# Last norm through VectorE's block transposes, a third output chunk on GpSimd, and other transfer prices in the ordering model

## The chip, the core and the metric

The kernel runs on one core of one Trainium2 chip. The core has five engines that run side by side, each with its own queue of instructions: PE (TensorE, matmuls into PSUM), DVE (VectorE), ACT (ScalarE), POOL (GpSimd) and SP (SyncE, which here issues nearly all transfers). They wait for each other through semaphores. The metric is the device time of one execution in microseconds; less is better.

## What is computed

Two layers of an encoder trunk on 512 tokens of width 1024, and a last RMSNorm. Cut to the parts that matter here:

```python
def rms_norm(x, g):
    x32 = x.astype(jnp.float32)
    y = x32 * lax.rsqrt(jnp.mean(x32 * x32, axis=-1, keepdims=True) + EPS)
    return (y * g.astype(jnp.float32)).astype(x.dtype)
...
    for l in range(DEPTH):
        x = x + hybrid_mixer(rms_norm(x, norm_mix[l]), ...)
        x = x + memory_cross_attention(rms_norm(x, norm_mem_q[l]), rms_norm(mem, norm_mem_kv[l]), ...)
        x = x + conv_ffn(rms_norm(x, norm_ffn[l]), w_up[l], conv_w[l], conv_b[l], w_down[l])
    return rms_norm(x, norm_final)
```

The mixer has neighbourhood attention and grouped-query attention side by side; conv_ffn ends in a product with w_down, 2816 by 1024. Everything is float32 outside; the products are made of three float32r products of high and low parts (mm3).

## The kernel before

The residual x is kept transposed: eight tiles xT of 128 channels by 512 tokens. A product is a run of matmuls of 128 by 128 weights on up to 512 columns. Weights come from memory into two "raw" buffers, are split into a high part (ACT) and a low part (POOL or DVE), and wait in four buffers until PE uses them. In the attention parts, the keys of two heads are doubled by a transfer inside the SBUF (line 998, "r<-r" in the profile), ahead of the scores that use them.

**The order.** The program does not run in the order in which it is written. Every instruction is first put on a tape (class Tape, lines 156 to 382); the tape knows what each one reads and writes. `plan` (line 344) then simulates the five engines with prices of its own: matmuls and elementwise work by columns (`times`, line 109), a transfer by 450 ns to issue it, its bytes by one of three rates (line 96), and LANDING, 1500 ns, until its result may be used (line 317). Each engine takes the step that is due first among those that can start soon; PE may run ahead of its written order by up to 300 steps. Three settings with three rounds each give nine orders. Each is then run again three times with random delays on every step (line 360), and the order with the best mean is played. So every engine's order, that of SP's queue too, follows from these prices. On the chip the queues are strictly in order: a step whose operand is late holds all behind it on its engine.

**A norm.** The squares of the eight chunks are summed on ACT and DVE or POOL into `acc`. Every norm but the last goes through `totals` (line 698): DVE transposes `acc` in blocks of 32 by 32, reduces within blocks, and PE adds across with the constant matrix `sel`; `by_block` scales in four pieces of 32 partitions, POOL takes the power -1/2 (`rsqrt`) and lays the values out with a mask (`apart`); later `along` multiplies with `sel` once more and DVE transposes the result, repeated, into a tile as wide as the tokens (`rep`).

The last norm has its own way. Its eighth square is kept apart (`last`, line 780), `stat` sums `acc` and `last` by matmuls with a column of ones (line 794), three blocks of 128 tokens each, and `spread` calls `row_rep` (line 737): three matmuls of the repeated scale with the identity give the wide tile in PSUM, and ACT copies it to the SBUF as `rep` for POOL, which does not read PSUM.

**The end** (`down_last`, lines 1595 to 1671). The first 384 tokens end in transposed layout, the last 128 ("tail") in rows of tokens. PE first makes all eight chunks for the 384 tokens; then two closing products of 512 columns for the tail, `pms[0]` and `pms[1]`. The norm's `stat` is written between their parts, `spread` after `pms[0]`. Eight multiplications by the wide scale follow, chunks 2 and 5 on POOL from `rep`, the others on DVE from PSUM, and after each one SP issues its output. Behind the last closing matmul come ACT's square with its sum, DVE's variance `v`, POOL's power `rstd`, the scaling of the two halves of `y` on DVE and ACT, and one output from each of SP and ACT.

Of the kernel before, what the change touches and what calls it, by code (L numbers as in the profile page):

```python
# [11 lines left out]
F32 = mybir.dt.float32  # L12
F32R = mybir.dt.float32r
AF = mybir.ActivationFunctionType
ALU = mybir.AluOpType
# [38 lines left out]

ENGINES = range(5)
E_PE, E_ACT, E_DVE, E_POOL, E_SP = ENGINES
HANDOVER, LANDING, IN_FLIGHT, GRACE = 40.0, 1500.0, 8, 140.0
IN_PSUM = ("mm", "sc", "tr")
TWO_INPUTS = ("tensor_add", "tensor_sub", "tensor_mul", "tensor_tensor", "scalar_tensor_tensor")
FAST = ("tensor_scalar", "tensor_copy")  # L60
# [15 lines left out]
class Step:  # L76
# [5 lines left out]
    def __init__(self, i, engine, name, call, args, kwargs):  # L82
        self.i, self.engine, self.name, self.call = i, engine, name, (call, args, kwargs)
        self.reads, self.writes = [], []
        for n, a in [*enumerate(args), *kwargs.items()]:
            if hasattr(a, "tensor") or type(a).__name__ == "Tile":
                a = a if hasattr(a, "ap") and not callable(a.ap) else a[:]
                (self.writes if n in (0, "out", "accum_out") else self.reads).append(a)
        self.needs, self.frees, self.after, self.leads = set(), set(), set(), set()
        self.opens, self.tiles, self.moved = [], [], 0  # L90
        if name == "dma_start":
            self.busy = self.length = 450.0
            to, source = self.writes[0], self.reads[0] if self.reads else None
            short = min(4 * a.ap[-1][1] for a in (to, source) if a is not None) < 1024
            inside = source is not None and type(source.tensor).__name__ == type(to.tensor).__name__ == "Tile"
            rate = 215.0 if to.shape[0] < P or inside else 300.0 if short else 370.0
            self.moved = 4 / rate
            for c in to.shape:
                self.moved *= c
        elif name == "make_identity":  # L100
            self.busy = self.length = 1200.0
        else:
            self.busy, self.length = self.times()
        ends = self.reads[:: max(1, len(self.reads) - 1)] if name in TWO_INPUTS else self.reads[:1] + self.writes
        self.shared = engine == E_POOL and columns(self.writes[0]) > 8 or (
            engine == E_DVE and (name in TWO_INPUTS or name in FAST and (name == "tensor_copy" or columns(self.writes[0]) > 4))
            and all(tag_of(a.tensor) not in IN_PSUM for a in ends))
# [48 lines left out]
class Tape:  # L156
# [84 lines left out]
    def run(self, due, rank, patience, ahead, margin=0.0, aside={}, order=None, rng=None):  # L241
# [32 lines left out]
        for _ in steps:  # L274
# [39 lines left out]
            end = t + busy + s.length - s.busy + late[i]  # L314
            if s.moved:
                memory = max(memory, t + busy) + s.moved
                end = memory + LANDING + 12.0 * late[i]
                flying.append(end)
            taken.append(i)
            open_to[s.engine].remove(i)  # L320
# [23 lines left out]
    def plan(self, log=None):  # L344

        n = len(self.steps)
        best = None
        for patience, ahead, margin, aside, rounds in PLANS:
            rank, at, now = list(range(n)), [0.0] * n, 0.0
            for s in self.steps:  # L350
                at[s.i] = now
                now += s.busy * (s.engine == E_PE)
            for _ in range(rounds):
                r = self.run(self.due(at, rank), rank, patience, ahead, margin, aside)
                if r is None:
                    if log:
                        log("stuck")
                    break
                at = r[1]
                under = [self.run(None, rank, (0.0,) * 5, 0, order=r[2], rng=np.random.default_rng(k)) for k in range(3)]  # L360
                mean = sum(u[0] if u else 1e9 for u in under) / len(under)
                if log:
                    log(r[0], mean)
                if best is None or mean < best[0]:
                    best = mean, r[2]
        return best[1]
# [104 lines left out]
def encoder_kernel(ctx: ExitStack, tc: tile.TileContext, t: dict, out: list):  # L471
# [16 lines left out]
    def nm(s):  # L488
        uid[0] += 1
        return f"{s}_{uid[0]}"  # L490
# [15 lines left out]
    def tmp(shape=(S,)):  # L506
        return tpool.tile([P, *shape], F32, tag="t", name=nm("t"))

    def small(n):
        return spool.tile([P, n], F32, tag="s", name=nm("s"), padded_shape=[P, 16])  # L510
# [184 lines left out]
    mhalf = cpool.tile([P, 8], F32, name="mhalf")  # L695
    DVE.memset(mhalf, -0.5)

    def totals(acc, n):


        t = tmp((n,))
        DVE.transpose(t, acc)
        part = small(n // 32)
        DVE.tensor_reduce(part, t.rearrange("p (j c) -> p j c", c=32), axis=AX.X, op=ALU.add)
        pv = ps_t()
        PE.matmul(pv[:, 0 : n // 32], sel, part, start=True, stop=True)
        return pv[:, 0 : n // 32]

    def by_block(v, nb, op):


        for a in range(4):
            q = slice(32 * a, 32 * a + 32)
            op(q, v[q].rearrange("p (b a) -> p a b", a=4)[:, a])
# [15 lines left out]
    def along(rep, e, n):  # L730
# [2 lines left out]
        pr = ps_t()[:, 0 : n // 32]  # L733
        PE.matmul(pr, sel, e, start=True, stop=True)
        DVE.transpose(rep.rearrange("p (j c) -> p j c", c=32), pr.unsqueeze(2).to_broadcast([P, n // 32, 32]))

    def row_rep(rstd, n, tag, bufs, copy):

        pr = ps_t()
        for b in range(n):  # L740
            PE.matmul(pr[:, b * P : (b + 1) * P], rstd[:, b : b + 1].to_broadcast([P, P]), ident,
                      start=True, stop=True)
        rep = tpool.tile([P, n * P], F32, tag=tag, name=nm(tag), bufs=bufs)
        copy(rep, pr[:, : n * P])
        return rep, pr[:, : n * P]

    class Norm:

# [39 lines left out]
        def stat(self, factor=1.0):  # L788
            nb = self.n // P

            def sums(sq):
                pv = ps_t()
                for b in range(nb):
                    PE.matmul(pv[:, b : b + 1], sq[:, b * P : b * P + P], ones, start=True, stop=True)
                return pv[:, 0:nb]

            if self.last is None:
                pv = totals(self.acc, self.n)
                self.var = small(nb)
                by_block(pv, nb, lambda q, x: DVE.tensor_scalar(  # L800
                    self.var[q], x, factor / D, EPS * factor, op0=ALU.mult, op1=ALU.add))
                self.rstd = rsqrt(self.var, nb)
                if self.gcol != G_MQ:
                    self.wide = apart(self.rstd, nb)
                return

            part, v, self.rstd = small(nb), small(nb), small(nb)
            DVE.tensor_scalar(part, sums(self.acc), 1.0 / D, EPS, op0=ALU.mult, op1=ALU.add)
            DVE.scalar_tensor_tensor(v, sums(self.last), 1.0 / D, part, op0=ALU.mult, op1=ALU.add)
            POOL.tensor_tensor(self.rstd, v, mhalf[:, :nb], op=ALU.pow)  # L810

        def spread(self):
            if self.last is None:
                self.rep = tpool.tile([P, self.n], F32, tag="rep", name=nm("rep"), bufs=1)
                along(self.rep, self.wide, self.n)
            else:
                self.rep, self.psum = row_rep(self.rstd, self.n // P, "rep", 1, ACT.copy)

    def split_psum(hi, lo, ps, scale=None):
        if scale is None:  # L820
# [45 lines left out]
    def mem_stat():  # L866

        acc = None
        for i in range(KC // 2):
            sq = tmp((2, MEMN))  # L870
            SP.dma_start(sq, t["memT"][i * 256 : (i + 1) * 256, :].rearrange("(k p) n -> p k n", p=P))
            yield
            ACT.activation(sq, sq, AF.Square)
            if acc is None:
                acc = sq
            else:
                POOL.tensor_add(acc, acc, sq)
        POOL.tensor_add(acc[:, 0], acc[:, 0], acc[:, 1])
        yield
        v = small(MB)  # L880
        by_block(totals(acc[:, 0], MEMN), MB, lambda q, x: DVE.tensor_scalar(
            v[q], x, 1.0 / D, EPS, op0=ALU.mult, op1=ALU.add))
        yield
        POOL.tensor_tensor(mem_rstd, v, mhalf[:, :MB], op=ALU.pow)
        along(mem_rep, apart(mem_rstd, MB), MEMN)
        yield
# [31 lines left out]
    for l in range(DEPTH):  # L918
# [676 lines left out]
        def down_last(g):  # L1595
# [60 lines left out]
            norm.spread()  # L1656
            for k in range(KC):
                xk = xT[k][:, cs]
                if k in (2, 5):
                    POOL.tensor_mul(xk, xk, norm.rep)  # L1660
                else:
                    DVE.tensor_mul(xk, xk, norm.psum)
                SP.dma_start(out[0][k * P : (k + 1) * P, :], xk)
# [1 line left out]
            squares(1)  # L1665
            DVE.tensor_scalar(v, sums[:, 1:2], 1.0 / D, part0, op0=ALU.mult, op1=ALU.add)
            POOL.tensor_tensor(rstd, v, mhalf[:, :1], op=ALU.pow)
            DVE.tensor_scalar(y[:, 0], y[:, 0], rstd, 1.0, op0=ALU.mult, op1=ALU.mult)
            SP.dma_start(out[1][:, 0:512], y[:, 0])
            ACT.activation(y[:, 1], y[:, 1], AF.Copy, scale=rstd)  # L1670
            ACT.dma_start(out[1][:, 512:D], y[:, 1])

        for g, (j0, nj) in enumerate(GROUPS):
            for j in range(j0 + (g > 0), j0 + nj):
# [99 lines left out]
```

## Time and profile before

| | us |
|---|---|
| median of three runs | 1327.1 |
| lowest and highest of them | 1326.02, 1327.68 |
| the profiled execution | 1326.05 |
| its span, first to last instruction | 1324.3 |
| TensorE's granted clock in it | 0.999 |

The profile is one execution. Its engines are named PE (matmuls), PEld (weight loads, beside PE), DVE, ACT, POOL and SP; a "q" behind a name is the engine's sequencer, which issues transfers. An entry such as "mm<-r,hi 128x512 x8" is a group of instructions by the names of the tiles that they write and read, with the shape and the count. All recorded work has line 376, where the tape is played, so groups are told apart by tiles. In a view by time the first number is the start in microseconds and the second the time until the group's last instruction ends; what stands in brackets is the idle time before it and what ended it. PE's ends are modelled: neighbouring matmuls overlap in the view, and the distance from one start to the next is the time that PE was held.

### The profile page before, as it was taken

What the parts mean: (1) busy time and instruction counts of PE and PEld (TensorE: products, weight loads), DVE (VectorE), ACT (ScalarE), POOL (GpSimd) and SP (SyncE); (2) the same over time, 40 slices, a digit from 0 to 9 for tenths busy, and PEclk for the clock granted to TensorE, in tenths of its full rate; (3) what the DMA queues carried; (4) which work ended last, traced back from release to release, by engine and by line L of the source; (5) the groups of instructions that cost most, each with busy time, mean ns of one, the idle gap of its engine ahead of it and who ended that gap; (6) DMA issues with size and microseconds to landing.
All of it is one profiled execution on the core that took longest, in us unless ns stands there. A gap on an engine that the chain in (4) does not pass through costs nothing.

```text
span 1324.3 us, 17771 instructions
## 1 busy us (share of the span) xinstructions
PE 1315.4 (99%) x6385; PEld 1107.4 (84%) x6385; DVE 931.2 (70%) x1651; ACT 678.8 (51%) x1229; POOL 688.6 (52%) x479
## 2 busy tenths in 40 slices
PE   9999999999999999999999999999999999999998
PEld 8888888888888888888888988888888888888897
DVE  7679895777993388178445898867779815862874
ACT  7776786654442243144437868865644423432441
POOL 3565866737444444444625657765454444444451
PEclk9999999999999999999999999999999999999999
DMA  7751324313333333333355522233143333333331
GB/s 239 217 168 49 96 64 94 98 55 103 97 96 96 96 96 88 106 122 88 99 159 160 144 64 80 72 89 96 48 119 100 99 96 96 92 89 106 96 112 64
DMA packets 198328, 137.29 MB, mean 104 GB/s; under 512 B 5217, under 2 KB 184929, under 8 KB 198241
## 3 DMA queue, kind: packets, MB, share of 16 engines
q1 hardware_dynamic: 197808, 135.77, 35.4%
q8 instruction: 51, 0.84, 0.3%
q10 hardware_dynamic: 432, 0.39, 0.1%
q14 instruction: 37, 0.30, 0.1%
HBM read 126.18 MB, written 2.10 MB: 97 GB/s over the span
## 4 chain that ended last, share of the span: by engine, by line
PE 96%; POOL 2%; DMA 1%; issue 0%; DVE 0%; ACT 0%; SPq 0%; POOLq 0%; ACTq 0%
PE mm L376 85%; PE sc L376 7%; PE tr L376 4%; POOL lo L376 1%; DMA r<-r 1%; POOL r L376 0%; POOL t L376 0%; POOL s L376 0%; DVE r L376 0%; ACT r L376 0%; DVE s L376 0%; ACT t L376 0%; ACT hi L376 0%; SPq L376 0%; DVE t L376 0%
## 5 line engine op out<-in xcount | busy, mean ns | idle before, releaser
L376 POOL TENSOR_TENSOR lo<-raw,hi 128x1024 fp32r<-128x1024 f32 (+2 forms) x268 | 510.0, 1913 | 492.6 <-ACT hi L376 462.5
L376 PE MATMUL mm<-xg,hi 128*128 128x512 f32 (+1 forms) x1730 | 535.0, 390 | 0.0
L376 ACT CAST hi<-raw 128x512 fp32r<-128x512 f32 (+2 forms) x276 | 227.2, 841 | 376.9 <-PE mm L376 341.6
L376 PEld LDWEIGHTS mm<-xg,hi 128*128 128x128 f32 x1730 | 322.4, 188 | 65.2 <-ACT hi L376 0.2
L376 PE MATMUL mm<-xg,lo 128*128 128x512 f32 (+1 forms) x865 | 336.9, 389 | 0.0
L376 PE MATMUL mm<-r,hi 128*128 128x512 f32 (+1 forms) x1056 | 332.7, 390 | 0.0
L376 DVE SCALAR_TENSOR_TENSOR t<-t,par,t 128x504 f32<-128x504 f32 (+1 forms) x352 | 287.7, 854 | 39.6 <-ACT t L376 37.5
L376 PEld LDWEIGHTS mm<-r,hi 128*128 128x128 f32 x1056 | 197.0, 188 | 39.1 <-ACT r L376 0.4
L376 PE MATMUL mm<-r,lo 128*128 128x512 f32 (+2 forms) x560 | 210.9, 377 | 0.0
L376 PEld LDWEIGHTS mm<-xg,lo 128*128 128x128 f32 x865 | 162.5, 188 | 33.8 <-DVE lo L376 0.3
L376 DVE TENSOR_TENSOR xT<-xT,mm 128x512 f32<-128x512 f32 (+1 forms) x56 | 36.9, 667 | 121.5 <-PE mm L376 121.5
L376 PEld LDWEIGHTS mm<-r,lo 128*128 128x128 f32 x560 | 105.2, 188 | 19.4
L376 PE MATMUL mm<-hi,xg 128*128 128x512 f32 (+1 forms) x384 | 108.2, 358 | 0.0
L376 POOL TENSOR_SCALAR t<-t,s 128x512 f32<-128x512 f32 (+1 forms) x112 | 67.0, 613 | 72.5 <-DVE s L376 63.9
L376 PE MATMUL sc<-r,r 128*128 128x256 f32 (+1 forms) x382 | 82.8, 335 | 1.6 <-DMA r<-r 1.6
L376 DVE TENSOR_TENSOR t<-mm,rep 128x512 f32<-128x512 f32 x88 | 60.1, 687 | 31.2 <-PE mm L376 30.9
L376 ACT ACTIVATE t<-sc,s,s 128x512 f32<-128x512 f32 (+1 forms) x96 | 67.8, 710 | 26.4 <-DVE s L376 25.8
L376 ACT ACTIVATE t<-t,par 128x512 f32<-128x512 f32 x88 | 71.3, 813 | 12.3 <-DVE t L376 11.9
L376 PEld LDWEIGHTS mm<-hi,xg 128*128 128x128 f32 x384 | 68.4, 189 | 9.4
L376 PE MATMUL tr<-ident,t 128*128 128x128 f32 x488 | 70.6, 272 | 0.4 <-DVE r L376 0.4
L376 PEld LDWEIGHTS tr<-ident,t 128*128 128x128 f32 x488 | 58.8, 140 | 12.3 <-POOL t L376 0.8
L376 PE MATMUL mm<-lo,xg 128*128 128x512 f32 (+1 forms) x192 | 68.2, 355 | 0.0
(129 smaller groups left out, 1499.4 us busy)
## 6 DMA issues: line engine op xcount, KB each, us to landing
raw<-in_w_up SPq DMA_DIRECT2D x88, 512.0 KB, 3.9
raw<-in_w_in SPq DMA_DIRECT2D x33, 512.0 KB, 4.2
raw<-in_w_down SPq DMA_DIRECT2D x23, 512.0 KB, 3.9
raw<-in_w_down SPq DMA_DIRECT2D x24, 448.0 KB, 3.7
raw<-in_w_mem_kv SPq DMA_DIRECT2D x16, 512.0 KB, 4.0
r<-r SPq DMA_DIRECT2D x30, 256.0 KB, 4.1
r<-in_bias SPq DMA_DIRECT2D x16, 384.0 KB, 6.2
raw<-in_w_out SPq DMA_DIRECT2D x8, 512.0 KB, 3.5
```

Of the source, the lines that this page charges most:

```text
L376: call(*args, **kwargs)
```

## The change

Four edits:

1. The last norm's `stat` uses `totals` like the others. `totals` takes several tiles of squares, transposes and reduces each on DVE, and lets PE add them in one PSUM tile. `spread` uses `along`, into a PSUM tile this time, which ACT then copies to `rep` as before. The matmuls with ones and `row_rep` go.
2. Of the eight last multiplications POOL does chunks 1, 4 and 6 in place of 2 and 5.
3. The last scaling is cut at 640 of 1024 columns in place of 512: DVE and SP's output take 640, ACT and its output 384.
4. In the ordering model LANDING is 1800 in place of 1500, the three rates are 205, 285 and 340 in place of 215, 300 and 370, a trial run adds up to 1500 ns at random to each transfer where it was twelve times a delay of up to 80 ns, and there are six trial runs per order in place of three.

```diff
-HANDOVER, LANDING, IN_FLIGHT, GRACE = 40.0, 1500.0, 8, 140.0
+HANDOVER, LANDING, IN_FLIGHT, GRACE = 40.0, 1800.0, 8, 140.0
...
-            rate = 215.0 if to.shape[0] < P or inside else 300.0 if short else 370.0
+            rate = 205.0 if to.shape[0] < P or inside else 285.0 if short else 340.0
...
-                end = memory + LANDING + 12.0 * late[i]
+                end = memory + LANDING + (12.0 * late[i] if rng is None else 1500.0 * rng.random())
...
-                under = [self.run(None, rank, (0.0,) * 5, 0, order=r[2], rng=np.random.default_rng(k)) for k in range(3)]
+                under = [self.run(None, rank, (0.0,) * 5, 0, order=r[2], rng=np.random.default_rng(k)) for k in range(6)]
...
-    def totals(acc, n):
+    def totals(n, *squares):
...
+        parts = []
+        for sq in squares:
+            t = tmp((n,))
+            DVE.transpose(t, sq)
+            parts.append(small(n // 32))
+            DVE.tensor_reduce(parts[-1], t.rearrange("p (j c) -> p j c", c=32), axis=AX.X, op=ALU.add)
+        pv = ps_t()[:, 0 : n // 32]
+        for i, part in enumerate(parts):
+            PE.matmul(pv, sel, part, start=i == 0, stop=i == len(parts) - 1)
+        return pv
...
-            part, v, self.rstd = small(nb), small(nb), small(nb)
-            DVE.tensor_scalar(part, sums(self.acc), 1.0 / D, EPS, op0=ALU.mult, op1=ALU.add)
-            DVE.scalar_tensor_tensor(v, sums(self.last), 1.0 / D, part, op0=ALU.mult, op1=ALU.add)
-            POOL.tensor_tensor(self.rstd, v, mhalf[:, :nb], op=ALU.pow)
+            pv = totals(self.n, self.acc, *([] if self.last is None else [self.last]))
+            self.var = small(nb)
+            by_block(pv, nb, lambda q, x: DVE.tensor_scalar(
+                self.var[q], x, factor / D, EPS * factor, op0=ALU.mult, op1=ALU.add))
+            self.rstd = rsqrt(self.var, nb)
+            if self.gcol != G_MQ:
+                self.wide = apart(self.rstd, nb)
...
             else:
-                self.rep, self.psum = row_rep(self.rstd, self.n // P, "rep", 1, ACT.copy)
+                self.psum = ps_t()[:, : self.n]
+                along(self.psum, self.wide, self.n)
+                ACT.copy(self.rep, self.psum)
...
-                if k in (2, 5):
+                if k in (1, 4, 6):
                     POOL.tensor_mul(xk, xk, norm.rep)
                 else:
                     DVE.tensor_mul(xk, xk, norm.psum)
...
-            DVE.tensor_scalar(y[:, 0], y[:, 0], rstd, 1.0, op0=ALU.mult, op1=ALU.mult)
-            SP.dma_start(out[1][:, 0:512], y[:, 0])
-            ACT.activation(y[:, 1], y[:, 1], AF.Copy, scale=rstd)
-            ACT.dma_start(out[1][:, 512:D], y[:, 1])
+            yf = y.rearrange("p i n -> p (i n)")
+            DVE.tensor_scalar(yf[:, :640], yf[:, :640], rstd, 1.0, op0=ALU.mult, op1=ALU.mult)
+            SP.dma_start(out[1][:, 0:640], yf[:, :640])
+            ACT.activation(yf[:, 640:], yf[:, 640:], AF.Copy, scale=rstd)
+            ACT.dma_start(out[1][:, 640:D], yf[:, 640:])
```

More of the change, by code (lines that the diff above doesn't have):

```diff
@@ L696, in encoder_kernel @@
     DVE.memset(mhalf, -0.5)
-    def totals(acc, n):
[L701 to L707, printed above, removed]
+    def totals(n, *squares):
[9 more added lines that the diff above has]
+        return pv
     def by_block(v, nb, op):
@@ L735, in along @@
         DVE.transpose(rep.rearrange("p (j c) -> p j c", c=32), pr.unsqueeze(2).to_broadcast([P, n // 32, 32]))
[L737 to L745, printed above, removed]
     class Norm:
@@ L789, in stat, with spread @@
             nb = self.n // P
[L791 to L795, printed above, removed]
-            if self.last is None:
[L798 to L805, printed above, removed]
-            part, v, self.rstd = small(nb), small(nb), small(nb)
-            DVE.tensor_scalar(part, sums(self.acc), 1.0 / D, EPS, op0=ALU.mult, op1=ALU.add)
-            DVE.scalar_tensor_tensor(v, sums(self.last), 1.0 / D, part, op0=ALU.mult, op1=ALU.add)
-            POOL.tensor_tensor(self.rstd, v, mhalf[:, :nb], op=ALU.pow)
-        def spread(self):
-            if self.last is None:
-                self.rep = tpool.tile([P, self.n], F32, tag="rep", name=nm("rep"), bufs=1)
+            pv = totals(self.n, self.acc, *([] if self.last is None else [self.last]))
[5 more added lines that the diff above has]
+                self.wide = apart(self.rstd, nb)
+        def spread(self):
+            self.rep = tpool.tile([P, self.n], F32, tag="rep", name=nm("rep"), bufs=1)
+            if self.last is None:
                 along(self.rep, self.wide, self.n)
             else:
-                self.rep, self.psum = row_rep(self.rstd, self.n // P, "rep", 1, ACT.copy)
+                self.psum = ps_t()[:, : self.n]
+                along(self.psum, self.wide, self.n)
+                ACT.copy(self.rep, self.psum)
     def split_psum(hi, lo, ps, scale=None):
@@ L880, in mem_stat @@
         v = small(MB)
-        by_block(totals(acc[:, 0], MEMN), MB, lambda q, x: DVE.tensor_scalar(
+        by_block(totals(MEMN, acc[:, 0]), MB, lambda q, x: DVE.tensor_scalar(
             v[q], x, 1.0 / D, EPS, op0=ALU.mult, op1=ALU.add))
```

## The prediction

> **What bounds the kernel now.** I read the page first: its span, the busy shares and the chain that ended last; then who PE (TensorE) waits for, the table of equal stretches, the chain around the one long wait, and last the end of the span in order of time.
>
> ```profile
> span 1324.3 us, 17771 instructions
> ...
> PE 1315.4 (99%) x6385; PEld 1107.4 (84%) x6385; DVE 931.2 (70%) x1651; ACT 678.8 (51%) x1229; POOL 688.6 (52%) x479
> ...
> PE mm L376 85%; PE sc L376 7%; PE tr L376 4%; POOL lo L376 1%; DMA r<-r 1%; POOL r L376 0%; POOL t L376 0%; POOL s L376 0%; DVE r L376 0%; ACT r L376 0%; DVE s L376 0%; ACT t L376 0%; ACT hi L376 0%; SPq L376 0%; DVE t L376 0%
> ```
>
> PE is busy in 1315.4 of 1324.3 us, and 96% of the chain is PE by the three PE entries. A microsecond of another engine's work is therefore worth nothing unless PE stands for it or it lies behind the last matmul; a microsecond of PE work is worth one, as long as what follows it keeps pace. PE is not busy in 8.9 us, and this is where they are:
>
> ```profile
> PE sc L376 <- DMA r<-r: 1.6, 1, 1.6
> PE tr L376 <- DVE ones L376: 1.0, 1, 1.0
> PE tr L376 <- DVE r L376: 0.4, 1, 0.4
> ```
>
> ```profile
> 66.22:99.32 33.10, 31.52 (x217) 28.76 (x216) 25.10 (x72) 24.57 (x63) 21.02 (x25) 1.00 0.59 168
> ```
>
> ```profile
> 1305.64 0.53 ACT L376 ACTIVATE t<-xT 128x384 f32<-128x384 f32 x1 [3.11 <-DVE xT L376]
> ...
> 1307.15 1.39 PE L376 MATMUL tr<-ones,t 128*128 128x1 f32 x12
> ...
> 1308.40 0.48 PE L376 MATMUL sc<-hi,r 128*128 128x512 f32 x1
> ...
> 1308.82 0.85 POOL L376 TENSOR_TENSOR s<-s,mhalf 128x3 f32<-128x3 f32 x1 [19.39 <-DVE s L376]
> ...
> 1314.18 0.83 PE L376 MATMUL tr<-ident,s 128*128 128x128 f32 x6
> ...
> 1314.77 3.68 PE L376 MATMUL sc<-r,r 128*128 128x512 f32 x15
> 1315.05 0.48 ACT L376 COPY rep<-tr 128x384 f32<-128x384 f32 x1 [2.26 <-PE tr L376]
> 1315.56 2.88 DVE L376 TENSOR_TENSOR xT<-xT,tr 128x384 f32<-128x384 f32 x6 [1.99 <-ACT rep L376]
> 1315.61 2.00 POOL L376 TENSOR_TENSOR xT<-xT,rep 128x384 f32<-128x384 f32 x2 [5.94 <-ACT rep L376]
> 1316.15 3.85 SPq L376 DMA_DIRECT2D out<-xT  x8
> 1318.48 0.60 ACT L376 ACTIVATE t<-sc 128x512 f32<-128x512 f32 x1 [2.95 <-PE sc L376]
> ...
> 1319.21 0.21 DVE L376 TENSOR_SCALAR s<-s,s 128x1 f32<-128x1 f32 x1 [0.77 <-ACT t L376]
> ...
> 1319.50 0.55 POOL L376 TENSOR_TENSOR s<-s,mhalf 128x1 f32<-128x1 f32 x1 [1.90 <-DVE s L376]
> 1320.09 0.48 DVE L376 TENSOR_SCALAR r<-r,s 128x512 f32<-128x512 f32 x1
> 1320.11 0.72 ACT L376 ACTIVATE r<-r,s 128x512 f32<-128x512 f32 x1 [0.94 <-POOL s L376]
> 1320.60 0.33 SPq L376 DMA_DIRECT2D out<-r  x1
> 1320.87 0.35 ACTq L376 DMA_DIRECT2D out<-r  x1
> ```
>
> The waits of PE sum to 3.0 us: 1.0 at the start for a memset, 1.6 in one matmul of scores for a copy inside the SBUF, 0.4 for a VectorE result. The stretch from 66.22 shows the same hole (33.10 less 31.52 is 1.6 us). The last matmul ends at 1314.77 + 3.68 = 1318.45, and the span's last 5.85 us are the tail: a square with its sum on ScalarE, the variance on VectorE, a power on GpSimd, two scalings side by side, two output transfers and the closing of the program. So 3.0 + 5.85 is the whole of the 8.9. What can be won: work taken from PE, 2.0 us of waits (the start is untouched), and some of the tail.
>
> **Part one, the last norm.** Removed on PE: the sums by a column of ones, twelve instructions that hold PE from 1307.15 to the next matmul at 1308.40, 1.25 us; and the spreading by the identity, six that hold it from 1314.18 to 1314.77, 0.59 us. Added on PE: two matmuls with sel as weights in totals and one in along, each a pair of instructions on 12 columns. The trace has such pairs with 16 columns:
>
> ```profile
> 964.44 0.29 PE L376 MATMUL tr<-s,sel 128*128 128x16 f32 x2
> 964.58 0.71 PE L376 MATMUL mm<-xg,hi 128*128 128x512 f32 x2
> ```
>
> A pair holds PE for 964.58 - 964.44 = 0.14 us, so three hold it for 0.42. The sum is 1.25 + 0.59 - 0.42 = 1.42 us of PE work less. It counts in full only if the new chain does not make PE or the outputs wait, and that chain is longer. Its prices:
>
> ```profile
> L376 DVE STREAM_TRANSPOSE t<-t 128x512 f32<-128x512 f32 x6 | 4.3, 711 | 0.2
> ...
> L376 DVE TENSOR_REDUCE s<-t 128x16 f32<-128x512 f32 x6 | 4.1, 681 | 0.1
> L376 DVE TENSOR_SCALAR s<-tr 32x4 f32<-32x4 f32 x24 | 3.8, 158 | 6.8 <-PE tr L376 6.5
> ...
> L376 DVE STREAM_TRANSPOSE t<-t 128x256 f32<-128x256 f32 x1 | 0.4, 446 | 0.0
> ```
>
> ```profile
> L376 POOL TENSOR_TENSOR s<-s,mask 128x16 f32<-128x16 f32 x4 | 0.9, 218 | 0.3
> ```
>
> A VectorE transpose or reduction of 384 columns is not in the trace; between 446 ns at 256 columns and 711 at 512 I take the middle, 0.58 us for the transpose, and below 0.68 (the 512-column reduction) 0.55 for the reduction. First half, from the last square: ScalarE ends it at 1305.64 + 0.53 = 1306.17; transpose and reduction bring 1307.3 (those of the other seven chunks' sum are done or fit before, since VectorE has little to do there); a pair on PE 1307.6; four small scalings of 32 partitions at 158 ns, 0.63 us, 1308.3; the power on three columns, 0.85 us as at 1308.82, and the masking, 218 ns, 1309.5 with handovers. It is needed when PE comes to the spreading, now 1314.18 less the 1.25 - 0.28 us saved ahead of it, 1313.2. The cover is 3.7 us of product matmuls; both new POOL steps and the eleven or so on VectorE are hidden by it. If the cover were gone, each would cost its own duration, 3.3 us in all after the square.
>
> Second half: the pair ends near 1313.5 with its write; a transpose from PSUM to PSUM, 0.58 us, is new; then the same ScalarE copy as before (0.48), and the multiplications begin at about 1314.65 where they began at 1315.56. They come 0.9 us earlier, while PE's end comes 1.42 earlier, at 1317.03: half a microsecond of slack is spent. Behind them queue the variance on VectorE, the power on GpSimd and, in SyncE's queue, the last output.
>
> **Part two, three chunks on GpSimd.** VectorE did six in 2.88 us, one each 0.46; five end at 1314.65 + 2.4 = 1317.05, and the variance comes at 1319.21 - 1.42 = 1317.8: 0.7 us of cover. GpSimd did two in 2.00 us; three end at 1317.7, and its power is wanted at 1319.50 - 1.42 = 1318.08: 0.4 us of cover. SyncE issues eight transfers in 3.85 us; begun 0.9 earlier, the last ends at 1319.1, where the last output is wanted at 1320.60 - 1.42 = 1319.2. It just fits, so I cost this part at nothing, with a bound of +0.5 (half a microsecond of spent slack) if every one of these estimates is short.
>
> The Trainium skill, Perfetto Trace Analysis, section Optimizing Scalar/DVE Operations, speaks against it: GpSimd's only port is one that VectorE also uses, under a lock, so work moved between these two might gain nothing. The rows do not bear it out for these instructions: the multiplications of both ran at once, six in 2.88 us beside two in 2.00.
>
> **Part three, 640 + 384 columns.** Now VectorE scales 512 in 0.48 us and its transfer is issued at 1320.60; ScalarE takes 0.72 and its transfer is issued at 1320.87, the later one. By columns, 384 on ScalarE are between 0.54 us (in proportion) and 0.72 (no gain); I take 0.62, a tenth less. VectorE's 640 are at most 0.60 in proportion, so its transfer is issued by 1320.72, still before ScalarE's at 1320.77.
>
> ```profile
> out<-r SPq DMA_DIRECT2D x1, 256.0 KB, 2.1
> out<-r ACTq DMA_DIRECT2D x1, 256.0 KB, 2.4
> ```
>
> They land at 1322.7 and 1323.3, so ScalarE's sets the end; an earlier issue and fewer bytes there can win no more than the 0.57 us between the two, and the other one then takes over. Value -0.1 us (the earlier issue alone), from 0 to -0.5. The tail's sum is -1.42 - 0.1 = -1.5 us, bounds -1.42 - 0.5 = -1.9 and -1.42 + 0.5 = -0.9.
>
> **Part four, the ordering model.** The landing price goes from 1500 to 1800 ns and the three rates fall by 5 to 8%; the trial runs are six and put up to 1500 ns of chance on each transfer. Nothing is computed differently, but every engine's order, SyncE's queue included, may come out new in the whole kernel. What the transfers really take:
>
> ```profile
> raw<-in_w_up SPq DMA_DIRECT2D x88, 512.0 KB, 3.9
> ...
> r<-r SPq DMA_DIRECT2D x30, 256.0 KB, 4.1
> r<-in_bias SPq DMA_DIRECT2D x16, 384.0 KB, 6.2
> ```
>
> The old model gives a 256 KB copy 450 + 1500 + 262144 / 215 = 3.17 us, the new one 3.53; the median row says 4.1. For a 512 KB load it was 3.37 and is 3.79; the row says 3.9. So the model came nearer to the rows, and what it places behind a transfer goes later by some 0.4 us. The stall it could mend is this one:
>
> ```profile
> 68.31 3.75 POOL lo L376 x3
> ...
> 72.08 0.37 SPq L376
> ...
> 72.62 7.17 DMA r<-r
> ```
>
> Read in order of time: GpSimd's three splits until 72.06, then the load on SyncE that waited for them, then the copy behind it in the same queue, 7.17 us until it lands, then PE's scores. The copy stood behind a load that waited for a buffer. If it goes ahead of it, or the scores go later among the projections, the 1.6 us vanish. The bounds are -2.0 us (this and the 0.4) and, on the other side, a stall of the same kind made new: 7.17 less the 3.53 that the model will grant is 3.6 us for one copy. I take -1.6: the one long wait is of exactly the sort of transfer whose price is raised, and PE stood for no other transfer in 1324 us.
>
> **Sum.** The profiled execution took 1326.05 us, of which 1324.3 are the span; -1.5 - 1.6 = -3.1 makes it 1322.95. The median of the runs shown, 1327.1, is 1.05 above that execution, and the change is the same for both: 1324.0. What the measurement can tell from no change is about 0.2%, 2.65 us here, so the bound of faster is 1324.45 and of slower 1329.75.
>
> **Rivals.** *The order is neutral.* A stall vanishes and as much appears elsewhere; only the tail counts: 1327.1 - 1.5 = 1325.6, within 0.2%. For it: the loads' prices were raised as well as the copies' (0.42 us against 0.36), so SyncE's order between the two need not turn round. Against it: the trial runs now punish an order that has no slack for a late transfer.
>
> *A new stall.* Another copy inside the SBUF, or a bias load (6.2 us by its row), ends up behind a load that waits for GpSimd, in the dense stretches where the queue is shared, and PE stands 3.6 us for it. One such stall and the old one kept give 1327.1 - 1.5 + 3.6 = 1329.2; two give 1332.8. It decides from 1.5 + 2.65 = 4.2 us of new waits on. For it: the whole order is drawn anew and the present one has just 2.0 us of mendable waits, so there is more to lose than to win. Against it: the present order came from a model that was further from the rows, and had only one such stall.
>
> *The outputs take over.* If VectorE's and GpSimd's multiplications excluded each other, eight would take 5 x 0.46 + 3 x 1.0 = 5.3 us from 1314.65, to 1319.95, and the power wanted at 1318.08 would come 1.9 us late: 1327.1 - 1.5 + 1.9 = 1327.5 without a gain from the order, a change that does not do what it says. Against it stand the two rows in which both ran at once; little chance. This is the case that the rule of the Trainium skill (Perfetto Trace Analysis, Optimizing Scalar/DVE Operations) would make, taken at its strictest.
>
> **Chances.** Forecast 0.56, of which 0.04 falls short of 2.65 us; neutral order 0.20; a new stall 0.19, of which 0.01 stays under the bound; the outputs 0.05. So faster 0.52, same 0.04 + 0.20 + 0.01 + 0.05 = 0.30, slower 0.18. The forecast's own range is 1323.2 to 1325.0 (the bounds -1.9 and -2.0 on the one side; -0.9 and -1.2, three quarters of the wait, on the other). The full range reaches down to 1321.6, by the spread of the runs shown (1327.68 - 1326.02 = 1.66), and up to 1329.2, the one new stall; about 0.15 is left out, nearly all above.
>
> **What would show it.** In the changed profile PE's instructions fall by 12 (twelve and six out, six in), the sel matmuls with 12 columns hold PE 0.14 us each, and PE's end to the span's end stays at 5.75. A multiplication on GpSimd that ends after ScalarE's last square begins, or a last output issued right behind the eight others, would show the fit of part two wrong. The scores' wait for the copy is absent, and PE's waits sum to about 1.4 us with the start; a PE wait for a transfer of 2 us or more anywhere makes the forecast wrong, and so does a chain through GpSimd's power of the norm.

## The result, and the profile after

| | before | after |
|---|---|---|
| median of six runs, us | 1327.76 | 1322.93 |
| lowest and highest | 1326.02, 1328.26 | 1322.43, 1324.17 |
| ratio, 95% interval | | 0.9973 (0.9962 to 0.9984) |
| the profiled execution, us | 1326.05 | 1324.17 |
| its span, us | 1324.3 | 1322.3 |

Faster by 0.27%, 3.6 us by the ratio. The medians of the table are 4.8 us apart, but before's six lie high: in the three later sessions its median was 1326.2 to 1326.9. The two profiled executions are 2.0 us of span apart, less than the medians: before's lies at the fast end of its six, after's is the slowest. Where that comes from is seen below. First the page of after:

```profile
span 1322.3 us, 17751 instructions
...
PE 1313.2 (99%) x6373; PEld 1105.8 (84%) x6373; DVE 936.4 (71%) x1657; ACT 675.2 (51%) x1229; POOL 691.9 (52%) x481
```

PE's instructions fell by the 12 that were expected. Who PE waited for, in after:

```profile
PE tr L376 <- DVE ones L376: 1.0, 1, 1.0
PE mm L376 <- ACT hi L376: 0.8, 1, 0.8
PE mm L376 <- ACT r L376: 0.4, 2, 0.2
PE tr L376 <- POOL lo L376: 0.3, 1, 0.3
PE sc L376 <- DVE xg L376: 0.3, 1, 0.3
```

The wait of 1.6 us for the copy inside the SBUF is gone, and the 0.4 us one for VectorE too. What is new is small, and the 0.8 and the 0.3 for `xg` fall in the first 25 us. The busy time of two stretches, of before and then of after (stretch, its length, PE's busy time and count, then the weight loads and the other engines):

```profile
0.00:25.00 25.00, 23.96 (x107) 20.26 (x108) 19.89 (x47) 18.78 (x39) 5.42 (x11) 1.00 0.91 278
25.00:100.00 75.00, 73.42 (x429) 64.09 (x428) 52.61 (x137) 53.97 (x130) 45.02 (x50) 1.00 0.66 183
```

```profile
0.00:25.00 25.00, 22.91 (x103) 18.79 (x104) 20.12 (x42) 18.43 (x39) 5.05 (x11) 1.00 0.93 287
25.00:100.00 75.00, 74.66 (x441) 65.87 (x440) 52.95 (x144) 54.53 (x134) 45.08 (x50) 1.00 0.62 180
```

From 25 to 100 us PE is busy for 74.66 in place of 73.42 us and does twelve instructions more. In the first 25 us after has 1.05 us less; but the run with 512 + 512 below, whose PE queue is the same from first to last, has this in its profile:

```profile
0.00:25.00 25.00, 23.96 (x108) 20.26 (x109) 20.63 (x45) 18.70 (x39) 5.59 (x11) 1.00 0.91 285
```

That is before's number exactly, in a program whose start is after's. So the first 25 us differ from one execution to the next by a microsecond, while PE waits for the first tiles to be split (the 0.8 and the 0.3 for `xg`), and the profiled execution of after had a slow one.

SyncE's queue around the copies, of before and then of after:

```profile
70.58 0.47 SPq L376 DMA_DIRECT2D r<-r  x1
72.08 0.37 SPq L376 DMA_DIRECT2D raw<-in_w_in  x1
72.62 0.73 SPq L376 DMA_DIRECT2D r<-r  x1
```

```profile
71.17 1.33 SPq L376 DMA_DIRECT2D r<-r  x2
72.59 1.72 SPq L376 DMA_DIRECT2D r<-in_bias  x2
75.46 0.38 SPq L376 DMA_DIRECT2D raw<-in_w_in  x1
```

In before a load stands between the two copies ("r<-r"). In after both copies are issued together, then the biases, then the next load. And the end of after, in order of time:

```profile
1306.06 0.29 PE L376 MATMUL tr<-s,sel 128*128 128x12 f32 x2
...
1306.20 0.48 PE L376 MATMUL sc<-hi,r 128*128 128x512 f32 x1
...
1306.52 0.40 PE L376 MATMUL sc<-lo,r 128*128 128x512 f32 x1
...
1308.98 0.21 POOL L376 TENSOR_TENSOR s<-s,mask 128x12 f32<-128x12 f32 x1
...
1312.25 0.29 PE L376 MATMUL tr<-s,sel 128*128 128x12 f32 x2
...
1312.39 3.69 PE L376 MATMUL sc<-r,r 128*128 128x512 f32 x15
...
1313.71 2.41 DVE L376 TENSOR_TENSOR xT<-xT,tr 128x384 f32<-128x384 f32 x5 [0.55 <-ACT rep L376]
1313.76 2.96 POOL L376 TENSOR_TENSOR xT<-xT,rep 128x384 f32<-128x384 f32 x3 [4.57 <-ACT rep L376]
1314.30 3.86 SPq L376 DMA_DIRECT2D out<-xT  x8
...
1317.13 0.55 POOL L376 TENSOR_TENSOR s<-s,mhalf 128x1 f32<-128x1 f32 x1 [0.40 <-DVE s L376]
...
1318.34 0.33 SPq L376 DMA_DIRECT2D out<-r  x1
1318.39 0.36 ACTq L376 DMA_DIRECT2D out<-r  x1
```

The last matmul ends at 1312.39 + 3.69 = 1316.08, 2.37 us earlier than in before. To see what of it the end alone won, take one mark that both have, the last pair of a norm in the second layer; before first, then after:

```profile
970.82 0.29 PE L376 MATMUL tr<-s,sel 128*128 128x16 f32 x2
```

```profile
969.72 0.29 PE L376 MATMUL tr<-s,sel 128*128 128x16 f32 x2
```

From the mark to PE's end before took 1318.45 - 970.82 = 347.63 us and after takes 1316.08 - 969.72 = 346.36: 1.27 us less PE work at the end. But the time from PE's end to the span's end grew from 5.82 us (5.85 with the span rounded to 1324.3) to 6.22, though the chain in it runs as before up to the two last issues: ScalarE's, the later one, starts 2.31 us after PE's end (before 2.42). In the six profiles with before's end this time is 5.81 to 5.83, in the three whose last scaling is cut at 640 behind all eight outputs it is 6.22 to 6.25, so 0.4 us is well beyond the scatter. It grew in the landing:

```profile
out<-r SPq DMA_DIRECT2D x1, 320.0 KB, 2.7
...
out<-r ACTq DMA_DIRECT2D x1, 192.0 KB, 2.9
```

Before these read 2.1 and 2.4 us. What the transfers find at their issue is in the table of stretches, in the 2.2 us ahead of it; before first, then after:

```profile
1318.45:1320.60 2.15, 0.00 (x0) 0.00 (x0) 1.30 (x3) 1.17 (x3) 0.55 (x1) 1.00 1.03 368
```

```profile
1316.10:1318.30 2.20, 0.00 (x0) 0.00 (x0) 1.38 (x4) 1.25 (x3) 1.17 (x2) 1.00 1.04 378
```

The DMA share (last but one) is 1.03 and 1.04: in both the sixteen engines are full with the chunks' outputs when the last two come. But in before SyncE's eighth issue ends at 1316.15 + 3.85 = 1320.00 and the last one starts 0.60 us later; in after it ends at 1314.30 + 3.86 = 1318.16 and the last one starts after 0.18. The last two come 0.42 us sooner behind the same backlog, and land about that much later.

### The profile page after: what moved, and what is told of

Same layout as the page of the kernel before. It is cut to its first block, busy times and chain, and to the rows that moved or that the text cites. A ratio compares the mean times of both kernels' runs of the same rounds, so it can differ in the third digit from the quotient of the medians.

```text
span 1322.3 us, 17751 instructions
## 1 busy us (share of the span) xinstructions
PE 1313.2 (99%) x6373; PEld 1105.8 (84%) x6373; DVE 936.4 (71%) x1657; ACT 675.2 (51%) x1229; POOL 691.9 (52%) x481
## 4 chain that ended last, share of the span: by engine, by line
PE 97%; ACT 1%; DVE 1%; POOL 0%; DMA 0%; issue 0%; SPq 0%; DVEq 0%; POOLq 0%; ACTq 0%
PE mm L376 86%; PE sc L376 6%; PE tr L376 4%; POOL lo L376 0%; DMA xT<-in_xT 0%; ACT hi L376 0%; ACT xg L376 0%; ACT t L376 0%; DVE r L376 0%; ACT r L376 0%; SPq L376 0%; DVE xg L376 0%; DVE t L376 0%; POOL t L376 0%; DVE s L376 0%
## 5 line engine op out<-in xcount | busy, mean ns | idle before, releaser
L376 DVE SCALAR_TENSOR_TENSOR t<-t,par,t 128x504 f32<-128x504 f32 (+1 forms) x352 | 281.3, 837 | 38.5 <-ACT t L376 36.5
```

The costliest lines, as they stand in the source:

```text
L376: call(*args, **kwargs)
```

## The experiments

Each is compared with before in the same session. All but one keep to the full computation.

**The end alone.** The changed kernel with the old prices (the rates too) and the old trial runs.

```diff
-HANDOVER, LANDING, IN_FLIGHT, GRACE = 40.0, 1800.0, 8, 140.0
+HANDOVER, LANDING, IN_FLIGHT, GRACE = 40.0, 1500.0, 8, 140.0
...
-                end = memory + LANDING + (12.0 * late[i] if rng is None else 1500.0 * rng.random())
+                end = memory + LANDING + 12.0 * late[i]
```

> Parts one to three (norm, three chunks on GpSimd, 640 + 384) with the old prices and three trial runs. Its order is that of before but for the end. Theory A (the parts add): PE's end comes 1.4 us sooner, so 1.5 us less than before, a ratio of 0.9989; the scores' wait of 1.6 us for the copy inside the SBUF stands as in before. Theory B (the order alone makes the gain, and what PE saves at the end is given back by the longer chain of the norm or by the outputs' landing): no gain, ratio 0.9998 to 1.0002.

Ratio 0.9995 (0.9986 to 1.0004), median 1326.39. The profile decides what the clock can't. PE's wait for the copies in this run:

```profile
PE sc L376 <- DMA r<-r: 1.3, 2, 1.0
```

From the mark (972.39 here) to PE's end (1318.74) are 346.35 us, after's number: the 1.3 us of PE work are saved. The landings are after's 2.7 and 2.9 us, and 6.2 us lie behind PE's end: 0.4 us are given back. By the profile the end is worth 0.9 us, between theory A's 1.5 and theory B's nothing; the wait for the copies stands, now in two pieces.

**The ordering model alone.** The kernel of before with all new prices and trial runs.

```diff
-HANDOVER, LANDING, IN_FLIGHT, GRACE = 40.0, 1500.0, 8, 140.0
+HANDOVER, LANDING, IN_FLIGHT, GRACE = 40.0, 1800.0, 8, 140.0
...
-                end = memory + LANDING + 12.0 * late[i]
+                end = memory + LANDING + (12.0 * late[i] if rng is None else 1500.0 * rng.random())
```

> Part four alone: the new prices and trial runs, with the old last norm, chunks 2 and 5 and 512 + 512. Theory A: the wait of 1.6 us and the 0.4 us one are gone and some small ones are new, 1.0 to 2.1 us less than before, ratio 0.9984 to 0.9992. Theory B: the whole gain of the change, ratio 0.9973, 3.6 us or more.

Ratio 0.9983 (0.9974 to 0.9991): 2.3 us, most of the change's gain. Two short waits in its profile are new:

```profile
PE mm L376 <- ACT r L376: 0.4, 2, 0.2
```

```profile
25.00:100.00 75.00, 74.64 (x445) 66.03 (x444) 53.97 (x145) 55.32 (x137) 44.82 (x50) 1.00 0.62 180
```

Beside these and the start's 1.0, PE waits twice for 0.4 us, for ScalarE and for GpSimd; it waits for no transfer. And from 25 to 100 us PE is busy 1.22 us more than in before. From the mark (968.47) to PE's end (1316.10) are 347.63 us, before's number. So the two halves of the change do separate things: this one brings the mark forward by 970.82 - 968.47 = 2.35 us, the other shortens what comes after it.

Where the 2.35 us come from can be read at an earlier mark, the pair of a norm that before starts at 81.59 us and this run at 79.03; up to it PE's queue holds the same matmuls in both, in another order. The stretches up to this mark and from it to the later one, of before and then of this run:

```profile
0.00:81.59 81.59, 78.97 (x390) 66.51 (x390) 56.98 (x136) 58.40 (x131) 41.58 (x48) 1.00 0.78 222
81.59:970.82 889.23, 888.80 (x4408) 747.73 (x4407) 640.40 (x1200) 492.67 (x934) 494.27 (x366) 1.00 0.33 95
```

```profile
0.00:79.03 79.03, 77.52 (x389) 65.94 (x390) 56.24 (x132) 56.97 (x128) 39.52 (x47) 1.00 0.73 220
79.03:968.47 889.44, 888.64 (x4407) 748.05 (x4406) 643.19 (x1205) 491.73 (x937) 498.07 (x368) 1.00 0.33 96
```

The whole gain lies ahead of the first mark, 2.56 us; behind it the new order is 0.21 us slower. Of the 2.56, 1.11 us are idle time of PE (2.62 less 1.51), and 1.45 us are time that the view counts as busy: the same matmuls take 77.52 in place of 78.97 us. What shortens that part was not taken apart.

**512 + 512, and chunks 2 and 5,** both in the changed kernel.

```diff
-            DVE.tensor_scalar(yf[:, :640], yf[:, :640], rstd, 1.0, op0=ALU.mult, op1=ALU.mult)
-            SP.dma_start(out[1][:, 0:640], yf[:, :640])
+            DVE.tensor_scalar(yf[:, :512], yf[:, :512], rstd, 1.0, op0=ALU.mult, op1=ALU.mult)
+            SP.dma_start(out[1][:, 0:512], yf[:, :512])
...
-                if k in (1, 4, 6):
+                if k in (2, 5):
```

> The changed kernel with the last scaling cut at 512 + 512 again. Theory A (the prediction's): ScalarE's half is issued 0.1 us later and carries more, so the time from PE's end to the span's end is 0.1 us longer than in the changed kernel, not to be told by the clock (same within 0.3 us). Theory C (the larger output of SyncE lands later and gives it back): that time is 0.2 to 0.4 us shorter, as in before (5.85 us where the changed kernel has 6.2).

> The changed kernel with chunks 2 and 5 on GpSimd again and six on VectorE. Theory A: VectorE's six take 2.9 us from 1313.7 and end at 1316.6, before the variance at 1316.84, so the third chunk on GpSimd was worth nothing: same within 0.2 us. Theory D: the variance, or the outputs behind the sixth multiplication, come later by up to 0.4 us and the end with them.

The cut at 512: 0.9976 (0.9966 to 0.9986), and 1321.07 - 1314.91 = 6.16 us from PE's end to the span's end: neither 0.1 longer nor 0.2 shorter than after's 6.22. So the cut at 640 gains nothing; by the profile it costs 0.06 us, hardly more than the scatter of 0.03. The chunks: 0.9979 (0.9970 to 0.9988), 1322.41 - 1316.16 = 6.25 us; again within 0.03 of after: the third chunk on GpSimd is worth nothing either, as theory A has it.

**One load put behind one copy.** Before's kernel in its own order, with the weight load of 72.08 placed behind the copy of 72.62 in the order that is played. The queues of PE, VectorE, ScalarE and GpSimd stay the same; SyncE's changes by these two.

```diff
-        for i in self.plan():
+        for i in one_load_later(self, self.plan()):
...
+    load = moves[moves.index(copy) - 1]
...
+    order.remove(load)
+    order.insert(order.index(copy) + 1, load)
```

> The kernel of before in its own order, but for one weight load that goes behind the copy inside the SBUF in SyncE's queue (the two at 72.08 and 72.62); every other queue is the same. Theory E (the wait of 1.6 us came from the copy standing behind a load that waits for its buffer): the copy is issued at about 71.3, lands before the scores at 78.2, the wait is gone and the excess of TensorE between 25 and 100 us falls by 1.2 to 1.6 us; ratio about 0.9989. Theory F (the copy is slow because the DMA engines are full there, whichever way round): the wait stays above 1 us, or the load's own user waits as long; ratio 1.000.

Ratio 0.9990 (0.9982 to 0.9999). SyncE's queue, PE's only new wait and the stretch from 25 to 100 us in this run:

```profile
69.87 1.25 SPq L376 DMA_DIRECT2D r<-r  x2
71.92 0.37 SPq L376 DMA_DIRECT2D raw<-in_w_in  x1
```

```profile
PE mm L376 <- DVE r L376: 0.4, 1, 0.4
```

```profile
25.00:100.00 75.00, 74.51 (x441) 65.34 (x440) 53.46 (x141) 54.84 (x137) 44.19 (x49) 1.00 0.62 180
```

The copies go together at 69.87 and PE no longer waits for one. PE is busy 74.51 us where it was 73.42, 1.1 us more, a little under the 1.2 to 1.6 that theory E expected. Most of what is missing is a new wait of 0.4 us for VectorE at 77.53 us, ahead of the scores that used to wait (78.34 here); its chain goes back through ScalarE to the load issued at 69.43, which landed after 4.57 us. Theory E holds, if at a little less: the 1.6 us came from one copy that stood behind one load.

**Half the outputs.** The changed kernel with the outputs of chunks 4 to 7 left out.

```diff
-                SP.dma_start(out[0][k * P : (k + 1) * P, :], xk)
+                if k < 4:
+                    SP.dma_start(out[0][k * P : (k + 1) * P, :], xk)
```

> The changed kernel, with outputs of chunks 0 to 3 alone; chunks 4 to 7 of the first output are computed but not written. Theory G (the last two outputs land 0.5 us later than in before because the chunks' outputs still fill the DMA engines): they land in 2.1 to 2.4 us again and the time from PE's end to the span's end falls from 6.2 to 5.8 us or less. Theory H (the later landing comes from the cut at 640 or from issuing the two within 0.05 us of each other): it stays at 6.1 to 6.2.

```profile
out<-r SPq DMA_DIRECT2D x1, 320.0 KB, 2.5
...
out<-r ACTq DMA_DIRECT2D x1, 192.0 KB, 2.6
```

The landings fall from 2.7 and 2.9 to 2.5 and 2.6 us, and PE's end lies 1320.86 - 1314.89 = 5.97 us before the span's end: 0.25 of the 0.4 us come back, not all. This is theory G's way, but short of its 5.8; most of the rest goes with the cut at 640, as a run further below shows.

**An early spreading.** The changed kernel with the norm's spreading ahead of the second closing product.

```diff
                     squares(i)
+                    norm.spread()
             part0, v, rstd = small(1), small(1), small(1)
...
-            norm.spread()
             for k in range(KC):
```

> The changed kernel with the norm's spreading written ahead of the second closing product, so that PE takes its pair of sel matmuls about 2.4 us sooner (the masked scale is ready at 1309.2). Theory G: the eight multiplications and their outputs start 2 us sooner, the DMA engines are empty when the last two outputs are issued, PE's end is unmoved and the span ends 0.4 us sooner: 0.4 us less than the changed kernel. Theory H: no gain, 6.2 us from PE's end to the span's end as before.

The end of this run in order of time (the eight outputs, the two last), the stretch in which the last two are issued, and the landings:

```profile
1312.01 3.81 SPq L376 DMA_DIRECT2D out<-xT  x8
...
1317.52 0.33 SPq L376 DMA_DIRECT2D out<-r  x1
1317.57 0.36 ACTq L376 DMA_DIRECT2D out<-r  x1
```

```profile
1317.50:1318.20 0.70, 0.00 (x0) 0.00 (x0) 0.00 (x0) 0.04 (x1) 0.00 (x0) 1.00 0.00 0
```

```profile
out<-r SPq DMA_DIRECT2D x1, 320.0 KB, 2.5
...
out<-r ACTq DMA_DIRECT2D x1, 192.0 KB, 2.6
```

The eight outputs are issued from 1312.01, 3.25 us ahead of PE's end where it was 1.78 in after, so 1.5 us sooner by that measure. The DMA share is 0.00 when the last two are issued: the backlog is gone, and they come into the same landings as with half the outputs left out. PE's end to the span's end is 1321.18 - 1315.26 = 5.92 us, 0.3 of the 0.4 us that theory G expected. Ratio 0.9977 (0.9969 to 0.9985): by the clock no different from after; the 0.3 us are seen in the profile alone.

**The prices one by one,** in the kernel of before: LANDING alone, the rates alone, the trial runs alone.

> The kernel of before with LANDING 1800 alone: old rates, old trial runs, old end. Its order differs from that of the new prices in about as many places as from that of before. Theory I (a dearer landing is what mends the order): ratio 0.998 to 0.999, no wait of PE for a transfer. Theory J (any change of price draws the order anew, and how good the draw is does not follow from the price): anything from 0.997 to 1.003, with waits in other places than in the two orders seen.

> The kernel of before with the three new rates alone. In SyncE's order the weight load still stands between the two copies. Theory I (the dearer landing mends the order): PE's wait for the copy stands, 1 to 2 us, ratio 0.9995 to 1.0005. Theory J (the draw): as likely as not 0.998, like the other redrawn orders.

> The kernel of before with the new trial runs alone (six, with up to 1500 ns of chance on each transfer); the prices that make the orders are the old ones. The weight load still stands between the two copies, and the order differs from before in 1125 lines of PE's queue. Theory I: PE's wait for the copy stands and the gain is less than 1 us, ratio 0.9993 or more. Theory J: anything, 0.997 to 1.003.

PE's only waits but the start's, of the run with the landing alone, then the rates' and the trial runs' one for copies:

```profile
PE mm L376 <- ACT r L376: 0.4, 2, 0.2
```

```profile
PE sc L376 <- DMA r<-r: 1.3, 1, 1.3
```

```profile
PE sc L376 <- DMA r<-r: 2.2, 3, 1.2
```

Landing: 0.9984 (0.9976 to 0.9992). Rates: 0.9998 (0.9989 to 1.0007). Trial runs: 0.9994 (0.9985 to 1.0002). In the runs with the dearer landing alone and with all new prices the load stands behind both copies; with the rates or the trial runs alone it stays between them, and PE waits 1.3 and 2.2 us for copies, as before did for 1.6.

How far were these orders drawn anew? Counted place by place in PE's queue of 6350 matmuls, the landing's order differs from that of all new prices in 1060 places, and it does as well; the trial runs' order differs from before's in 1004, and the rates' in only 119. So theory I is borne out as far as these orders go: both real redraws with 1800 put the load behind the copies, the one real redraw without it does not, and the rates alone hardly redraw anything. Theory J is not excluded by so few draws. Landing prices such as 1700 or 2000 were not tried, and why the dearer landing gains more than the one wait is open.

**Early spreading with 512 + 512,** with all new prices and with the landing as the only one.

> The changed kernel with the early spreading and 512 + 512 columns. Theory G (the last outputs wait only for the chunks' outputs, and the cut is worth nothing): 5.7 to 5.9 us from PE's end to the span's end, 0.3 to 0.5 us less than the changed kernel, the same as with the early spreading and 640 within 0.15. Theory K (640 + 384 does pay once the DMA engines are free): 0.1 us or more longer than with the early spreading and 640, above 6.0 us.

> The same with LANDING 1800 as the only new price (old rates, old trial runs): the order of the run with the landing alone, but for the end. If the parts add, the ratio is that run's 0.9984 less 1.4 us of PE work, 0.9973, and the run-to-run spread is as small as that run's, under 1 us; against it, the two orders of the middle may be equal and nothing is won or lost to the changed kernel.

Ratios 0.9970 (0.9960 to 0.9981) and 0.9974 (0.9963 to 0.9984). The landings of the first of them:

```profile
out<-r SPq DMA_DIRECT2D x1, 256.0 KB, 2.0
out<-r ACTq DMA_DIRECT2D x1, 256.0 KB, 2.4
```

These are before's within 0.1, and PE's end lies 1321.66 - 1315.85 = 5.82 us before the span's end, in the second 5.81. So 0.3 of the 0.4 us were the backlog of the chunks' outputs and 0.1 goes with the cut at 640 of 1024. Whether that 0.1 comes from the unequal sizes or from issuing the two 0.05 us apart (0.26 with 512 + 512) was not separated. Theory G holds, K does not. This version is the best end of all that ran, by the profile; by the clock it can't be told from after. The second, whose order is that of the run with the landing alone but for the end, spreads from 1322.62 to 1324.73, so the small spread of that run (1323.99 to 1324.73) was not the order's doing.

## Why the prediction was right, and where it was off

1324.0 us was forecast, faster, and 1322.93 was measured. That lies 0.3 us below the forecast's own range (1323.2 to 1325.0) and inside the full one. The forecast of -3.1 us stands beside -3.6 by the ratio (-2.1 to -5.0), and beside the sum of the halves measured apart by the profile, -2.35 for the order's mark and -1.27 + 0.4 for the end, -3.2. Step by step:

- **PE work less, 1.42 us:** 1.27. The pairs hold PE 0.14 us as the row said (1306.06 to 1306.20), but the matmul behind such a pair starts its next one 0.32 us later (1306.20 to 1306.52) and not 0.23. Behind the removed sums it was the same (1308.40 to 1308.72 in before), but three pairs now stand where two groups stood: that makes one more 0.09, most of the missing 0.15.
- **The longer chain is hidden:** right. The masked scale was ready at 1309.2 and PE took it at 1312.25; the multiplications begin 2.37 us before PE's end, where the prediction had 1317.03 - 1314.65 = 2.38 us.
- **Three chunks on GpSimd at nothing:** right for the engines. GpSimd ends at 1313.76 + 2.96 = 1316.72, its power starts at 1317.13; SyncE's eighth issue ends at 1318.16, its last one starts at 1318.34. The port's rival fell: three on GpSimd in 2.96 us and five on VectorE in 2.41 ran at once, each at the pace of before. The Trainium skill (Perfetto Trace Analysis, Optimizing Scalar/DVE Operations) says that moving work between the two might not help because of a shared port; in these multiplications, where VectorE has one operand in PSUM, no stretch shows.
- **"It just fits, so I cost this part at nothing, with a bound of +0.5":** this is the step that failed. The issues fit in SyncE's queue, but the prediction took the landings of before for the last outputs, and these now came 0.42 us sooner behind eight outputs that had the DMA engines full. The half microsecond of spent slack was given back nearly whole, 0.4 us. It was priced as a bound and not as the value. ScalarE's own queue did not save its output, which landed after 2.9 us. The Trainium skill (DMA: Bandwidth & Descriptors, Issuing engines are not separate DMA queues) says that transfers of all issuing engines run on the same sixteen DMA engines and interleave; the 2.9 us agree.
- **640 + 384 for -0.1 us:** nothing. ScalarE's output was issued 0.11 us sooner, as forecast, and the landing took it back; the cut costs about 0.1 once the DMA engines are free (2.5 and 2.6 us of landing against 2.0 and 2.4).
- **The order for -1.6 us:** the one wait went, by the mechanism that was forecast, but it is worth only 1.1 of the 2.35 us, as the swap shows. The 0.4 us wait near 144 us is gone too, but the two new ones of 0.2 us (at 286 and 938 us) stand against it. The other 1.25 us were in no term of the prediction: they lie ahead of 82 us, in time that counts as busy for PE, and their cause is open. Single profiles carry their start with them (the last section), so the sizes are good to about a microsecond; the clock says 2.3 us (1.2 to 3.4).
- **PE's waits would sum to 1.4 us:** 2.8 in the profiled execution of after, with 0.8 and 0.3 in its slow first 25 us; 2.2 in the run of the order alone (1.0 and three of 0.4).

Two errors of opposite sign, 0.6 us too much for the end and 0.75 too little for the order, made the sum come out. That the total fits so well is luck; the direction is not, and the saved work at the end and the one wait are shown by runs of their own.

## What to carry to other kernels

Where PE is busy 99% of the span, look for the one wait that is left and follow it back to the queue it stood in: here one load ahead of one copy in SyncE's queue was worth a microsecond, and the order that came of a dearer landing in the model, nearer to the measured one, no longer had it. At the end of a kernel, count the bytes that are still to go out from the first output on, not only the issues: if the DMA engines are full when the last output is issued, an earlier end of the computation is partly given back, and earlier first outputs are worth more than a better cut of the last ones.

## What was not expected of the hardware

The first 25 us of the same instruction queues take a microsecond more or less from one execution to the next (22.91 and 23.96 us of PE's busy time with one PE queue). Six profiles (after, and the runs with 512 + 512, with chunks 2 and 5, with half the outputs, and with the early spreading at 640 and at 512) have the same order up to the last norm. They reach the first pair of `sel` matmuls between 24.03 and 25.28 us, and the mark in the second layer between 968.53 and 969.81: the 1.25 us of the start are carried, unchanged, through the whole run. It fits the spread of 1322.43 to 1324.17 over the six runs of after, though runs without a profile do not show their start. What sets it was not settled.
